# Two-layer streaming-encoder trunk on one core: the second layer's values projected token-major for four heads at a time

## The chip, the core and the metric

The kernel runs on one core of a Trainium2 chip. The metric is the device time of one execution in microseconds (us). The engines work side by side and wait for one another on semaphores: PE (TensorE) multiplies matrices, DVE (VectorE) and ACT (ScalarE) work element by element, POOL (GpSimd) clears buffers and issues some DMAs, SP (SyncE) issues the others. A matmul of PE takes a stationary operand of 128 x 128, which a separate load puts in place (PEld in the profile), and a moving operand of up to 512 columns, which streams past it; the product is summed in PSUM, which has eight banks of 128 x 512 float32.

## The reference, cut to what matters

The model has two layers over 512 tokens of width 1024. The change lies at the border between them: after the first layer the keys and values that the second layer reads are projected from the normalised stream, and each of 12 heads of width 64 attends over all earlier chunks.

```
ks_, vs_ = jnp.split(rmsnorm(x, kv_norm_g) @ w_kv, 2, axis=-1)      # (512, 1024) @ (1024, 1536)
...
s = jnp.einsum('bqhd,bkhd->bhqk', qc, kc).astype(jnp.float32) * scale + bias
s = jnp.where(valid, s, -jnp.inf)
p = jax.nn.softmax(s, axis=-1).astype(vc.dtype)
return jnp.einsum('bhqk,bkhd->bqhd', p, vc)
...
def rmsnorm(x, g):
    y = x32 * lax.rsqrt(jnp.mean(x32 * x32, axis=-1, keepdims=True) + EPS)
    return (y * g.astype(jnp.float32)).astype(x.dtype)
```

The factor of the norm is one number per token, so it can be applied to a projection's output in place of its input. The kernel does that: the input of the projection, `kvact`, holds x times the gain `kv_norm_g` only.

## The kernel before

**Numbers in two parts.** Every matmul operand is held as a high and a low part (`split`, L139: ACT casts the high part, L140; DVE subtracts it from the source, L141). A product is three matmuls, high by high, high by low, low by high (`mm3`, L192 to L196), summed in one PSUM bank.

**The stream is held feature-major.** `xT[j]`, j = 0 to 7, has 128 features on the partitions and the 512 tokens along the columns. A projection (`project`, L198) makes 128 output features by 512 tokens: it loads the weights' 128 columns for all eight feature blocks (512 KB, one DMA on SP's queue into a `wr` buffer), casts them into two weight tiles, and runs 8 steps of `mm3` with the weights stationary and the 512 tokens moving. One "step" below is one `yield` of this loop: three matmuls of 512 columns.

**Weight tiles** (`weight_tiles`, L160). There are three blocks, 0, 1 and 2, each a `wh` and a `wl` tile. Without an argument the blocks are taken in turn (`turn[0]`); with `block=` a given one is taken. Blocks 0 and 1 have 64 bytes (`HALF`, 16 floats) to spare, and which end is left free depends on the caller:

```
at = HALF if i < 2 and (block is None) == (tag == "wh") else 0
```

Counted in units of 64 bytes and in the order of the tags in `sizes` (L82 to L84), a tile of tag `u` begins at an even unit, `wh0` and `wh1` at an odd one, `wl0` and `wl1` at an even one. So weights that are taken in turn lie at even units, like `u`; weights with `block=` given lie at odd units, 64 bytes off `u`. The forms of the first layer's channel mixer use `block=0` and `block=1` (L903, L906) and multiply by activations in `u`, with the weights stationary.

**The border between the layers.** The last part of the first layer's down projection runs in a loop over j = 0 to 7 (L1283): weights of 128 x 768 from the rotating blocks, 18 matmuls of 512 columns, the sum added to `xT[j]`, its squares added to the norm's sum, and two scaled copies in two parts each, `kvact[j]` and `act[j]`, all in `u` tiles. `u` has 50 tiles, of which these 32 stay in use. Then `norm.finish` (L291) makes `norm.row`: 128 equal rows of 512, the norm's factor of each token; it is given projection steps to run beside it.

**The second layer's mixer.** A generator named `fill` runs six calls of `project_pair(j)` (two heads each), with the two memory-query projections before and after the sixth. In `project_pair` there are 24 steps: 8 for the values' projection `ov`, 8 for the keys', 8 for the queries'. The values come out feature-major, while the attention needs them with the tokens on the partitions. So DVE multiplies `ov` by `norm.row` (`times_row`, L1312) into a `t` tile, PE turns it by four transposes of 128 x 128 into a PSUM bank (L1323), and two `split`s write it into two tiles of 128 x 512 (L1328): for each head 64 columns of high part and 64 of low part. The tiles are one `fh` and one `fl` (four of each) for pairs 0 to 4, and two `u` for pair 5. Queries go through `queries` (L569) into four `u` tiles, keys through `head_keys` (L531) into two.

`band_attention(j)` (L1333) has 10 stages: scores and softmax for each of four groups of tokens, transposes of the probabilities, products with the values. `weave` (L225) lets a given number of `fill` steps run between its stages: 1.68, 1.826, 1.633 and 1.848 for pairs 0 to 3, 3.456 for pair 4; `until` runs `fill` until a pair is there. After pair 3 `load_memory_kv(1)` (L546) puts four more tiles into `u`, and `memory_attention` 0 waits for the memory queries (four `u`). Later the output projection's parts take the place of `fill`, beside memory attention 1 and pair 5.

PSUM's banks are tagged: three `mm` for projections, three `sc`, two `tr`.

**Order.** In the channel mixers and the first stage the order on PE, ACT and DVE is written by hand (`manual_schedule`). In the border and the second mixer it is not: a planner places each instruction by the program's order as its priority and by a model of when operands and free tiles will be there, and the order of each engine is then fixed. Instructions marked `pin` keep their order.

Of the kernel before, what the change touches and what calls it, by code (L numbers as in the profile page):

```python
# [10 lines left out]
F32R = mybir.dt.float32r  # L11
I32 = mybir.dt.int32
AF = mybir.ActivationFunctionType
ALU = mybir.AluOpType
AX = mybir.AxisListType

P = 128
D = 1024
S = 512
# [30 lines left out]
def f(ap):  # L50
    return ap.bitcast(F32)
# [3 lines left out]
def trunk(  # L55
# [34 lines left out]
    def sb(tag, shape, dtype=F32):  # L90
        count[0] += 1
        return pool.tile(shape, dtype, tag=tag, name=f"{tag}{count[0]}", bufs=bufs[tag])

    def ps(tag):
        count[0] += 1
        return psum.tile([P, S], F32, tag=tag, name=f"p{tag}{count[0]}", bufs=pbufs[tag])
# [42 lines left out]
    def split(hi, lo, src, on_act=True, pinned=False):  # L139
        high = A.copy(hi, src) if on_act else V.tensor_copy(hi, src)  # L140
        low = V.tensor_tensor(out=lo, in0=src, in1=f(hi), op=ALU.subtract)  # L141
        if pinned:
            pin(high)
            pin(low)

    def load(src, a, b, extra=None):
        n = b + (extra.shape[-1] if extra is not None else 0)
        raw = sb("wr", [P, D])[:, : a * n].rearrange("p (a b) -> p a b", a=a)
        if isinstance(src, list):
            for i, one in enumerate(src):  # L150
                nc.sync.dma_start(raw[:, i, :], one)
        else:
            nc.sync.dma_start(raw[:, :, :b], src)
        if extra is not None:
            nc.sync.dma_start(raw[:, :, b:], extra)
        return raw
# [17 lines left out]
    def parts(raw, pinned=False, block=None):  # L174
        _, a, b = raw.shape
        hi, lo = weight_tiles(a, b, block)
        split(hi, lo, raw, pinned=pinned)
        return hi, lo
# [6 lines left out]
    def weights(*args):  # L185
        return parts(load(*args))

    def rows(w, c0, n, k0=0, k1=None):
        k1 = k1 if k1 is not None else w.shape[0] // P
        return w[k0 * P : k1 * P, c0 : c0 + n].rearrange("(k p) c -> p k c", p=P)  # L190

    def mm3(o, lh, ll, rh, rl, first, last, more=False):  # L192

        nc.tensor.matmul(o, lh, rh, start=first, stop=False, skip_group_check=more)  # L194
        nc.tensor.matmul(o, lh, rl, start=False, stop=False, skip_group_check=more)  # L195
        nc.tensor.matmul(o, ll, rh, start=False, stop=last, skip_group_check=more)  # L196

    def project(w, c0, act, tag="mm"):  # L198


        n = len(act)
        wh, wl = weights(rows(w, c0, P), n, P)
        o = ps(tag)
        for k in range(n):
            mm3(o, wh[:, k, :], wl[:, k, :], act[k][0], act[k][1], k == 0, k == n - 1)
            yield
        return o
# [323 lines left out]
    def head_keys(t):  # L531
        ks = [sb("u", [P, S], F32R) for _ in range(2)]
        for h, r in enumerate(HEADS):
            A.copy(ks[h][r, :], t[r, :])
            V.tensor_tensor(out=ks[h][HEADS[1 - h], :], in0=t[r, :], in1=f(ks[h])[r, :], op=ALU.subtract)
        return ks
# [744 lines left out]
    logarithms()  # L1281
    norm2, kvact, act = Norm(), [], []
    for j in range(KT):  # L1283
        wh, wl = weights(rows(ffn_w_down[0], j * P, P, FT - LAST, FT), LAST, P)
        o = ps("mm")
        for k in range(LAST):
            mm3(o, wh[:, k, :], wl[:, k, :], *hid[k], k == 0, k == LAST - 1)
        V.tensor_add(xT[j], xT[j], o)
        norm2.add(xT[j])
        kvact.append(scaled(xT[j], col["gkv"][:, j : j + 1]))  # L1290
        act.append(scaled(xT[j], col["gmix"][:, 8 + j : 9 + j]))
        G.dma_start(xspill[j], xT[j])
# [12 lines left out]
    def blocks(pt, o, step, n):  # L1305
        a = pt[:, o : o + P]
        return bass.AP(tensor=a.tensor, offset=a.offset, ap=[list(a.ap[0]), [step, n], [1, P]])

    def project_pair(j):
        def times_row(o):  # L1310
            t = sb("t", [P, S])
            V.tensor_tensor(out=t, in0=o, in1=norm.row, op=ALU.mult)  # L1312
            return t

        ov = yield from project(w_kv, AW + j * P, kvact)
        t = times_row(ov) if norm.row is not None else None
        o = yield from project(w_kv, j * P, kvact)
        if t is None:
            t = times_row(ov)
        k = head_keys(times_row(o))  # L1320
        tp = ps("mm")
        for T in range(TT):
            nc.tensor.transpose(tp[:, T * P : (T + 1) * P], t[:, T * P : (T + 1) * P], ident)  # L1323
        v = []
        for i in range(2):

            w = sb("u" if j == 5 else ("fh", "fl")[i], [P, S], F32R).rearrange("p (h c) -> p h c", h=4)
            split(w[:, :, :HD], w[:, :, HD:], tp[:, i * MEM : (i + 1) * MEM].rearrange("p (h c) -> p h c", h=4))  # L1328
            v += [w[:, :2, :], w[:, 2:, :]]
        q = queries((yield from project(b_w_in, j * P, act)), norm.row)  # L1330
        qkv[j] = q, k, v

    def band_attention(j, q, k, v):  # L1333
        pts = [sb("pt", [P, 5 * S], F32R) for _ in range(2)]
# [203 lines left out]
```

## Time and profile before

| | |
|---|---|
| median of three runs | 1180.86 us (1180.71 to 1181.27) |
| the profiled execution | 1181.04 us, with a span of 1179.3 us from first to last instruction |
| last products of the first channel mixer end | about 581.5 us |
| down-projection loop, j = 0 to 7 | about 577.5 to 613.4 us |
| first and last of the values' transposes (L1323) | 625.1 and 749.5 us |
| first scores of the second mixer's band attention | about 634 us |
| last products with the values | 803.7 us |

The page of the profile gives, for each engine, the time in which it was busy and its share of the span. Matmuls are pipelined: one of 512 columns is listed with about 390 ns, and the next begins about 227 ns after it, so the price of a matmul is read from the distance between starts, not from its own duration. Idle time is listed with what ended it; idle time of an engine that is not the bottleneck costs nothing.

### The profile page before, as it was taken

To read this page: it belongs to the slowest core of one execution; us is meant where nothing else is said; L and a number is where in the kernel's file an instruction comes from. 1 tells how busy PE (TensorE), PEld (TensorE's weight loads), DVE (VectorE), ACT (ScalarE), POOL (GpSimd) and SP (SyncE) were. 2 spreads that over 40 slices of the span, in tenths; PEclk is the share of its full clock that TensorE was granted. 3 is DMA by queue.
4 is the path that set the end of the run, shared out by engine and by line. 5 is a ranking of instruction groups with operands and counts; after the bars stand their busy time and mean duration, and the time that the engine had idled before them with its cause. 6 is when DMAs were issued, how large, how long until landed. Compare 5 with 4: busy or idle time off the path is not lost.

```text
span 1179.3 us, 18676 instructions
## 1 busy us (share of the span) xinstructions
PE 1169.1 (99%) x7007; PEld 1034.2 (88%) x7007; DVE 935.7 (79%) x1688; ACT 725.8 (62%) x1294; POOL 129.9 (11%) x222
## 2 busy tenths in 40 slices
PE   9999999999999999999999999999999999999997
PEld 9988888888889999999888888888889999999986
DVE  6877788887978877777698888897897877777755
ACT  6548677654655655555666667776565655555545
POOL 1111101000021111111020000101001011111100
PEclk9999999999999999999999999999999999999999
DMA  8645325244266677765564312335426466666551
GB/s 299 208 109 134 94 55 152 76 139 121 90 166 163 164 164 162 164 148 129 150 200 125 90 54 85 106 102 177 139 90 153 108 143 144 143 143 141 123 158 72
DMA packets 200156, 158.64 MB, mean 135 GB/s; under 512 B 8344, under 2 KB 179838, under 8 KB 200066
## 3 DMA queue, kind: packets, MB, share of 16 engines
q1 hardware_dynamic: 183906, 119.74, 34.6%
q0 software_dynamic: 15584, 36.67, 16.4%
q8 instruction: 55, 0.90, 0.3%
q10 hardware_dynamic: 576, 1.05, 0.2%
q14 instruction: 35, 0.29, 0.1%
HBM read 128.89 MB, written 32.46 MB: 137 GB/s over the span
## 4 chain that ended last, share of the span: by engine, by line
PE 94%; DVE 3%; ACT 1%; issue 0%; DMA 0%; SPq 0%; POOL 0%; ACTq 0%; POOLq 0%; DVEq 0%
PE pmm L194 18%; PE pmm L195 18%; PE pmm L196 18%; PE ptr L195 6%; PE ptr L194 6%; PE ptr L196 6%; PE psc L195 5%; PE psc L196 5%; PE psc L194 5%; PE psc L544 2%; PE ptr L1365 1%; PE ptr L1386 1%; PE ptr L1387 1%; PE ptr L627 1%; PE ptr L613 0%; DVE pt L141 0%
## 5 line engine op out<-in xcount | busy, mean ns | idle before, releaser
L194 PE MATMUL pmm<-u,wh 128*128 128x512 f32 (+1 forms) x968 | 333.2, 345 | 0.4 <-ACT u L140 0.2
L196 PE MATMUL pmm<-u,wl 128*128 128x512 f32 (+1 forms) x968 | 330.8, 342 | 0.0
L195 PE MATMUL pmm<-u,wh 128*128 128x512 f32 (+1 forms) x968 | 330.5, 342 | 0.0
L141 DVE TENSOR_TENSOR wl<-wr,wh 128x1024 fp32r<-128x1024 f32 (+3 forms) x172 | 199.6, 1162 | 101.8 <-ACT wh L140 101.4
L140 ACT CAST wh<-wr 128x1024 fp32r<-128x1024 f32 (+3 forms) x172 | 172.0, 1002 | 92.7 <-PE pmm L195 39.0
L196 PEld LDWEIGHTS pmm<-u,wl 128*128 128x128 f32 x968 | 181.9, 188 | 20.6
L194 PEld LDWEIGHTS pmm<-u,wh 128*128 128x128 f32 x968 | 181.8, 188 | 19.3 <-ACT u L140 1.1
L195 PEld LDWEIGHTS pmm<-u,wh 128*128 128x128 f32 x968 | 182.0, 188 | 18.5 <-DVE u L141 0.5
L194 PE MATMUL ptr<-u,wh 128*128 128x512 f32 x272 | 106.7, 392 | 0.0
L195 PE MATMUL ptr<-u,wh 128*128 128x512 f32 x272 | 106.5, 392 | 0.0
L196 PE MATMUL ptr<-u,wl 128*128 128x512 f32 x272 | 105.8, 389 | 0.0
L778 POOL DMA_DIRECT2D xspill<-t x64 | 55.6, 869 | 447.3 <-ACT t L777 437.5
L141 DVE TENSOR_TENSOR fl<-pt,fh 128x512 fp32r<-128x512 f32 x102 | 70.3, 689 | 11.2 <-ACT fh L140 8.5
L194 PE MATMUL pmm<-u,fh 128*128 128x256 f32 x272 | 75.4, 277 | 0.0
L195 PE MATMUL pmm<-u,fh 128*128 128x256 f32 x272 | 75.2, 276 | 0.0
L196 PE MATMUL pmm<-u,fl 128*128 128x256 f32 x272 | 75.2, 276 | 0.0
L195 PE MATMUL psc<-u,wh 128*128 128x256 f32 (+1 forms) x232 | 75.1, 324 | 0.0
L196 PE MATMUL psc<-u,wl 128*128 128x256 f32 (+1 forms) x232 | 75.1, 324 | 0.0
L194 PE MATMUL psc<-u,wh 128*128 128x256 f32 (+1 forms) x232 | 75.0, 324 | 0.0
L140 ACT CAST fh<-pt 128x512 fp32r<-128x512 f32 x102 | 62.7, 615 | 13.5 <-DVE pt L888 13.3
L950 ACT ACTIVATE t<-t 128x512 f32<-128x512 f32 x34 | 21.5, 632 | 79.2 <-DVE t L685 79.2
L777 ACT COPY t<-ptr 128x512 f32<-128x512 f32 x64 | 37.6, 587 | 51.6 <-PE ptr L196 51.6
(335 smaller groups left out, 2540.3 us busy)
## 6 DMA issues: line engine op xcount, KB each, us to landing
wr<-in_ffn_w_up_dram SPq DMA_DIRECT2D x54, 512.0 KB, 5.0
wr<-in_ffn_w_down_dram SPq DMA_DIRECT2D x38, 512.0 KB, 4.1
pt<-in_ffn_w_up_dram SPq DMA_DIRECT2D x34, 512.0 KB, 6.9
xspill<-t POOLq DMA_DIRECT2D x64, 256.0 KB, 4.7
wr<-in_a_w_in_dram SPq DMA_DIRECT2D x20, 512.0 KB, 3.8
wr<-in_w_kv_dram SPq DMA_DIRECT2D x12, 512.0 KB, 4.0
xspill<-fh POOLq DMA_DIRECT2D x16, 256.0 KB, 2.6
xspill<-fl POOLq DMA_DIRECT2D x16, 256.0 KB, 3.0
```

The source lines that it names most:

```text
L140: high = A.copy(hi, src) if on_act else V.tensor_copy(hi, src)
L141: low = V.tensor_tensor(out=lo, in0=src, in1=f(hi), op=ALU.subtract)
L194: nc.tensor.matmul(o, lh, rh, start=first, stop=False, skip_group_check=more)
L195: nc.tensor.matmul(o, lh, rl, start=False, stop=False, skip_group_check=more)
L196: nc.tensor.matmul(o, ll, rh, start=False, stop=last, skip_group_check=more)
L544: nc.tensor.matmul(o, a, b, start=first and i == 0, stop=i == 1)
L627: nc.tensor.matmul(o2, vs[a][:, 2 * hp + h, :], p[h][:, a, :], start=i == 0, stop=i == 3)
L777: A.copy(t, o)
L778: G.dma_start(xspill[j], t, accum_op=ALU.add)
L950: A.activation(self.acc, self.acc, AF.Silu)
L1365: nc.tensor.transpose(tp[:, b * P : (b + 1) * P], es[T, h][:, b * P : (b + 1) * P], ident)
L1386: nc.tensor.matmul(o2[:, s * P :], w, hi_at(pts[h], s, s, TT - s), start=s == 0, stop=False)
```

## The change

In place of one feature-major projection of the values for each pair of heads there is `token_values(g)`, called for pairs 0, 2 and 4, which projects the values of four heads (256 columns of `w_kv`) at once with the tokens on PSUM's partitions. The activations `kvact` are the stationary operand, 128 tokens at a time, and the weights move past in 256 columns. Two `mm` banks hold the four groups of tokens, two in each. The weights are two loads of 128 x 1024, given to blocks 0 and 1 by name, and stay there for both halves of the 16 steps; a step is now two `mm3` of 256 columns. The tokens now lie on the partitions, so the norm's factor is needed as a column: once, four `tensor_tensor_reduce` multiply `norm.row`'s blocks of 128 x 128 by the identity and sum each row, into `acol`, a tile of the first layer. ACT then writes the high part scaled by that column, and DVE the low part, straight from PSUM into four tiles: `fh` for the first call, `fl` for the second, `u` for the third. The transposes, the multiplication by the row and the bank for them are gone. In the down-projection loop the turn of the blocks is moved on by one at j = 1 and j = 3.

```diff
     for j in range(KT):
+        turn[0] += j in (1, 3)
         wh, wl = weights(rows(ffn_w_down[0], j * P, P, FT - LAST, FT), LAST, P)
...
+    vcol, vals = [], []
+
+    def token_values(g):
+
+        banks = [ps("mm").rearrange("p (i c) -> p i c", i=2) for _ in range(2)]
+        ws = []
+        for i in range(2):
+            for k in range(KT):
+                if i == 0 and k % 4 == 0:
+                    ws.append(parts(load(rows(w_kv, AW + g * MEM, MEM, k, k + 4), 4, MEM), block=k // 4))
+                wh, wl = ws[k // 4]
+                for b, o in enumerate(banks):
+                    T = 2 * i + b
+                    lh, ll = (t[:, T * P : (T + 1) * P] for t in kvact[k])
+                    mm3(o[:, i, :], lh, ll, wh[:, k % 4, :], wl[:, k % 4, :], k == 0, k == KT - 1)
+                yield
+        if not vcol:
+            vcol.append(acol[:, 0, :])
+            for T in range(TT):
+                V.tensor_tensor_reduce(
+                    out=sb("t", [P, S])[:, :P], in0=norm.row[:, T * P : (T + 1) * P], in1=ident, scale=1.0, scalar=0.0,
+                    op0=ALU.mult, op1=ALU.add, accum_out=vcol[0][:, T : T + 1],
+                )
+        vals.append([])
+        for T in range(TT):
+            w = sb(("fh", "fl", "u")[g], [P, S], F32R).rearrange("p (h c) -> p h c", h=4)
+            c, o = vcol[0][:, T : T + 1], banks[T % 2][:, T // 2, :].rearrange("p (h c) -> p h c", h=4)
+            A.activation(w[:, :, :HD], o, AF.Copy, scale=c)
+            V.scalar_tensor_tensor(w[:, :, HD:], o, c, f(w[:, :, :HD]), op0=ALU.mult, op1=ALU.subtract)
+            vals[g].append(w)
+
     def project_pair(j):
-        def times_row(o):
-            t = sb("t", [P, S])
-            V.tensor_tensor(out=t, in0=o, in1=norm.row, op=ALU.mult)
-            return t
-
-        ov = yield from project(w_kv, AW + j * P, kvact)
-        t = times_row(ov) if norm.row is not None else None
+        if j % 2 == 0:
+            yield from token_values(j // 2)
         o = yield from project(w_kv, j * P, kvact)
-        if t is None:
-            t = times_row(ov)
-        k = head_keys(times_row(o))
-        tp = ps("mm")
-        for T in range(TT):
-            nc.tensor.transpose(tp[:, T * P : (T + 1) * P], t[:, T * P : (T + 1) * P], ident)
-        v = []
-        for i in range(2):
-
-            w = sb("u" if j == 5 else ("fh", "fl")[i], [P, S], F32R).rearrange("p (h c) -> p h c", h=4)
-            split(w[:, :, :HD], w[:, :, HD:], tp[:, i * MEM : (i + 1) * MEM].rearrange("p (h c) -> p h c", h=4))
-            v += [w[:, :2, :], w[:, 2:, :]]
+        t = sb("t", [P, S])
+        V.tensor_tensor(out=t, in0=o, in1=norm.row, op=ALU.mult)
+        k = head_keys(t)
         q = queries((yield from project(b_w_in, j * P, act)), norm.row)
-        qkv[j] = q, k, v
+        qkv[j] = q, k, [w[:, j % 2 * 2 : j % 2 * 2 + 2, :] for w in vals[j // 2]]
```

## The prediction, made before the changed kernel was seen

> **What bounds the kernel now.** I read the page first, then the busy time by stage, the starts of single matmuls, the groups by line and shape, and the waits of PE's weight loads.
>
> ```profile
> span 1179.3 us, 18676 instructions
> ...
> PE 1169.1 (99%) x7007; PEld 1034.2 (88%) x7007; DVE 935.7 (79%) x1688; ACT 725.8 (62%) x1294; POOL 129.9 (11%) x222
> ...
> PE 94%; DVE 3%; ACT 1%; issue 0%; DMA 0%; SPq 0%; POOL 0%; ACTq 0%; POOLq 0%; DVEq 0%
> ```
>
> PE is busy 99% of the span and 94% of the chain that ended last. The busy time by stage (columns: window, its length, busy us of PE, weight loads, DVE, ACT, POOL; then clock and DMA) says the same of the stretches that the change touches: from the last down product to the first attention, the attentions of pairs 0 to 3, and the rest of the mixer.
>
> ```profile
> 613.00:641.00 28.00, 28.00 (x134) 23.33 (x133) 22.41 (x46) 15.85 (x31) 4.71 (x9) 1.00 0.46 141
> 641.00:742.00 101.00, 100.90 (x517) 84.44 (x516) 83.82 (x205) 68.10 (x148) 6.26 (x12) 1.00 0.30 89
> 742.00:806.00 64.00, 63.42 (x343) 51.80 (x342) 57.15 (x153) 48.23 (x123) 6.04 (x11) 1.00 0.33 100
> ```
>
> PE is full in all three; DVE follows with 80%, 83% and 89%. So a change here is worth what it takes from PE's stream, as long as DVE and the chains of the softmax keep up. How much PE waits there is in the waits of its weight loads from 614 to 812 us (waiting, on whom, us, times, longest):
>
> ```profile
> PEld ptr L613 <- issue: 1.0, 4, 0.4
> PEld ptr L1365 <- issue: 1.0, 4, 0.4
> PEld ptr L1365 <- DVE pt L141: 0.7, 2, 0.4
> PEld psc L544 <- ACT t L601: 0.6, 2, 0.5
> PEld ptr L1386 <- DVE pt L141: 0.6, 2, 0.3
> PEld ptr L627 <- DVE pt L141: 0.5, 1, 0.5
> ```
>
> The six longest sum to 4.4 us. There is little waiting for the change to remove, and covered waiting that it could uncover.
>
> **Removed from PE: the transposes.** Starts of PE's matmuls around the first group:
>
> ```profile
> 624.83 0.39 PE L196 MATMUL pmm<-u,wl 128*128 128x512 f32 x1
> 625.06 0.60 PE L1323 MATMUL pmm<-ident,t 128*128 128x128 f32 x4
> 625.42 0.47 PE L194 MATMUL pmm<-u,wh 128*128 128x512 f32 x1
> 625.73 0.39 PE L195 MATMUL pmm<-u,wh 128*128 128x512 f32 x1
> ...
> L1323 PE MATMUL pmm<-ident,t x24: 270/273/273, 625.1 to 749.5; 128*128 128x128 f32 x24
> ```
>
> From 624.83 to 625.73 lie two matmuls of 512 columns and four transposes; the first matmul after the transposes is late, as 0.31 us lie behind its start. Plain matmuls of 512 columns follow at
>
> ```profile
> 609.81 0.39 PE L195 MATMUL pmm<-u,wh 128*128 128x512 f32 x1
> ...
> 613.89 0.39 PE L195 MATMUL pmm<-u,wh 128*128 128x512 f32 x1
> ```
>
> 4.08 us for 18, 0.2267 us each. So a group costs 0.90 - 0.45 = 0.45 us, and six (24 transposes) 2.7 us. This is the gain that I am surest of.
>
> **Changed on PE: the products.** Six projections of 24 matmuls of 512 columns (144) become three calls of 96 of 256 (288): the same columns, twice the instructions and weight loads. No matmul of before has these operands at these places, so I bound the price from two sides (first and last of a run):
>
> ```profile
> 570.66 0.28 PE L194 MATMUL pmm<-u,wh 128*128 128x256 f32 x1
> ...
> 577.47 0.40 PE L194 MATMUL pmm<-u,wh 128*128 128x512 f32 x1
> ...
> 1170.00 0.28 PE L194 MATMUL pmm<-wh,u 128*128 128x256 f32 x1
> ...
> 1172.04 0.28 PE L196 MATMUL pmm<-wh,u 128*128 128x256 f32 x1
> ```
>
> In the channel mixer's step, weights stationary and 64 bytes off the moving `u`, 60 matmuls take 6.81 us: 113.5 ns, half of 227. In the last stage the activations are stationary and the weights move, as in the change, but both lie at even units: 17 take 2.04 us, 120 ns. The change has the roles of the second and the offset of the first. I take 113.5 ns: what differs between the rows besides the roles is the offset, and it should not matter which of two operands is the odd one. Then 288 x 113.5 ns = 32.7 us against 144 x 226.7 ns = 32.6 us: nothing. At 120 ns it is 34.6 us, 1.9 us more; that end stays for the range. The Trainium skill, "TensorE: Matmul & The Clock Gate", section "Back-to-back issue gap", gives N / 2.4 + 2.5 ns between matmuls of N columns, a fixed part that speaks against halving them; my estimate by it is 144 x 2.5 ns = 0.4 us more. The rows show no such part: 113.5 is half of 227.
>
> **DVE, ACT, SP.**
>
> ```profile
> L1312 DVE TENSOR_TENSOR t<-pmm,rb 128x512 f32<-128x512 f32 x12 | 8.2, 681 | 1.2 <-PE pmm L196 1.1
> L1350 DVE CUSTOM_DVE_ANT_0 t<-psc,bias 128x128 f32<-128x128 f32 x12 | 3.4, 286 | 0.7 <-PE psc L544 0.6
> L1350 DVE DVE_READ_ACCUMULATOR2_ANT s<- 128x1 f32 x48 | 3.9, 82 | 0.0
> L141 DVE TENSOR_TENSOR fh<-pmm,fh 128x256 fp32r<-128x256 f32 x5 | 2.1, 420 | 0.1
> L140 ACT CAST fh<-pmm 128x256 fp32r<-128x256 f32 x5 | 1.9, 374 | 0.1
> ...
> wr<-in_w_kv_dram SPq DMA_DIRECT2D x12, 512.0 KB, 4.0
> ```
>
> Six of the twelve multiplications by the row go: 4.1 us of DVE. Four reductions come, by the attention's own of that shape 4 x (286 + 82) ns = 1.5 us, once. The evictions stay twelve of 128 x 256 on each engine, now with a scale: 374 and 420 ns, with no row for a dearer form; twice that would be 9.5 us over both engines, spread over three calls. Weight loads and casts stay six of 512 KB on SP, two in a bunch where one came per pair. All this lies beside PE. Without that cover the four reductions and four evictions, about 1.5 + 4 x 0.42 = 3.2 us, would hold the queries' projection of pair 0, which needs one of the two `mm` banks: three banks, two held by the call, the third by the keys. The keys' 8 steps last 8 x 3 x 0.227 = 5.4 us, so it is covered. The reductions wait for `norm.row`, which comes when the eleventh of the sixteen steps is through, as `norm.finish` yields 7.4 and 4; behind them on DVE stand these evictions and the next weight subtraction, which has 5.4 us. The keys of pair 0 come after the row.
>
> **The turn of the blocks.** Products 2, 3 and 4 of the down loop now reuse the block of the product but one before, so their cast cannot run two ahead. It does not now:
>
> ```profile
> 586.85 0.83 ACT L140 CAST wh<-wr 128x768 fp32r<-128x768 f32 x1
> 587.08 0.69 DVE L1288 TENSOR_TENSOR fh<-fh,pmm 128x512 f32<-128x512 f32 x1 [0.81 <-DMA fl<-xspill]
> ...
> 589.57 0.82 ACT L140 CAST wh<-wr 128x768 fp32r<-128x768 f32 x1
> 589.75 0.68 DVE L1288 TENSOR_TENSOR fh<-fh,pmm 128x512 f32<-128x512 f32 x1
> ```
>
> The third cast starts as the first product's sum is added, the fourth as the second's is. I take nothing; were each of the three late by its cast, 0.8 us, it would be up to 2.5 us. In the second channel mixer's first projections the turn moves likewise, with 5.4 us for each cast.
>
> **Steps moved.** The fill has 160 steps before and after, but pair 0 now needs 32 and not 24. So attention 0 starts 8 steps, 5.4 us, later, and these are missing as cover later. How many arrive there is a matter of `u` tiles. Before, at memory attention 0, 32 (`kvact`, `act`) + 8 (four outputs) + 6 (pair 4) + 4 (`load_memory_kv`) = 50 are in use, and its queries need 4 more, which come free when the keys of pair 5 have used `kvact` 0 and 1:
>
> ```profile
> 736.59 0.69 DVE L574 SCALAR_TENSOR_TENSOR t<-pmm,rb 128x512 f32<-128x512 f32 x1
> ...
> 741.12 0.52 POOL L524 MEMSET u<- 64x512 f32 x1 [22.14 <-PE pmm L195]
> 741.37 0.63 ACT L525 ACTIVATE u<-t 64x512 fp32r<-64x512 f32 x1
> ...
> 742.02 0.62 ACT L528 CAST u<-u 64x512 fp32r<-64x512 f32 x1
> ...
> 742.70 0.38 PE L544 MATMUL psc<-u,u 128*128 128x256 f32 x1
> ```
>
> The queries are out of PSUM at 736.6, the first clear waits until 741.1, the scores start at 742.7. After, the third call has put four more tiles into `u`, so pair 4's queries wait too, and ahead of the memory's: ACT has 2 x (two of 0.63 us and two copies like them) = 5 us to do where 2.5 sufficed. Memory attention 0 then starts with some 15 of the 160 steps left in place of about 20. Those 5 steps, 3.4 us, are PE work done earlier, not lost: the stretch from 742 runs beside less of the projections and more of the output projection's parts, which do not depend on them. DVE has 1.5 us less to do there (pair 5's row 0.68, two evictions 0.84). I put down 0.2 us of new waiting, with -1 and +5.4 us as ends.
>
> **Sum:** -2.7 + 0 + 0.2 = -2.5 us against 1181.04 us of the profiled execution (span 1179.3 and 1.7 around it) is 1178.5. That execution lies 0.2 above the median of 1180.86, so I predict **1178.4 us**, with 1177.4 to 1179.4 for this case alone. What a measurement of this kernel can tell from no change is about 0.2%, 2.4 us: the forecast lies on that line.
>
> **Rivals.**
> 1. *The offset does nothing with the roles exchanged.* The row at 1170 us speaks for it: these are its roles, at 120 ns. Against: there the units agree. +1.9: 1180.3 us, the same within what can be told.
> 2. *DVE's relief shows.* 2.6 us less DVE where it is busy 83 to 89%, and half of the 4.4 us of PE's waits go as well: 1176.2 us. Against: most of these waits are on the attention's own steps.
> 3. *The cover is missing at the end: slower.* Place: memory attention 0 to the attention of pair 5. If pair 4's queries hold the queue of ACT and the softmax chains then run at their own pace, the 8 steps moved stand as idle PE time: 5.4 us, 1178.4 + 5.2 = 1183.6 us. It decides from 2.7 us of new waiting on. For it: DVE at 89% there, and `u` full. Against: the parts of the output projection can be pulled forward.
> 4. *The load of the stationary operand sets the spacing.* It takes 188 ns in the row below; were it not hidden, 288 x (188 - 113.5) ns = 21.5 us come on top: 1199.9 us. Against: the 60 matmuls at 113.5 ns have loads of the same length.
>
> ```profile
> L195 PEld LDWEIGHTS pmm<-u,fh 128*128 128x128 f32 x272 | 51.1, 188 | 1.2
> ```
>
> The same section of the Trainium skill says that loads and matmuls together set the spacing, 81 ns at 128 columns and 131 at 512; my estimate between them, 98 ns at 256, would make the change 9 us slower. The trace does not agree: 227 ns at 512, 113.5 at 256.
>
> **How the numbers follow.** Forecast 0.42, split by the line into 0.26 faster and 0.16 the same; rival 1 0.10, the same; rival 2 0.19, faster; rival 3 0.26, of which 0.02 the same and 0.24 slower; rival 4 0.03, slower. Faster 0.45, the same 0.28, slower 0.27. The range goes from 1175.2, 1 us beyond rival 2, to 1184.8, 1.2 us beyond rival 3; rival 4 and a longer loss stay outside.
>
> **What would show it.** Right: no rows of L1323; the 288 matmuls 113 to 114 ns apart; PE as busy as now from the first step to 806 us; all later stages 2 to 3 us earlier. Wrong: 120 ns between them (rival 1); PE idle before products with the values or transposes after memory attention 0, waiting for DVE or ACT (rival 3); a gap at the third to fifth down product (the turn); the queries of pair 0 waiting for a bank.

## The result, and the profile after

The changed kernel takes 1182.91 us (median of 22 runs, 1181.87 to 1183.74), the kernel before 1181.00 us in the same runs (1180.37 to 1183.07). The ratio is 1.0015, with a 95% interval of 1.0008 to 1.0022: 1.9 us slower, where 2.5 us faster was forecast. The time lies inside the predicted range and on the other side of no change. The profiled execution took 1182.67 us, with a span of 1181.0 us.

From the page of the kernel after, its span, the busy times and the chain that ended last:

```profile
span 1181.0 us, 18909 instructions
...
PE 1168.3 (99%) x7127; PEld 1038.9 (88%) x7127; DVE 933.9 (79%) x1690; ACT 725.9 (61%) x1294; POOL 129.2 (11%) x222
...
PE 92%; ACT 3%; DVE 3%; issue 1%; DMA 0%; SPq 0%; POOL 0%; DVEq 0%; ACTq 0%; POOLq 0%
```

PE has 0.8 us less to do than before (1169.1), and yet the span is 1.7 us longer: work went, and more waiting came. Where it came stands in the busy time by stage, in the three stretches of the prediction:

```profile
613.00:641.00 28.00, 28.00 (x173) 25.19 (x172) 19.73 (x36) 14.82 (x23) 4.71 (x9) 1.00 0.47 147
641.00:742.00 101.00, 100.92 (x610) 88.86 (x609) 85.60 (x219) 68.83 (x156) 6.06 (x12) 1.00 0.33 101
742.00:806.00 64.00, 61.32 (x328) 49.48 (x327) 56.00 (x150) 47.70 (x122) 5.77 (x11) 1.00 0.24 71
```

Up to 742 us PE is as full as it was. From 742 to 806 us it is busy for 61.32 us in place of 63.42: 2.1 us of new idle time. The waits of the weight loads from 614 to 812 us, the seven longest:

```profile
PEld psc L544 <- ACT u L528: 1.1, 1, 1.1
PEld ptr L613 <- issue: 1.0, 2, 0.8
PEld ptr L1383 <- issue: 1.0, 4, 0.5
PEld psc L544 <- DVE s L1368: 0.9, 1, 0.9
PEld psc L544 <- ACT pt L140: 0.9, 1, 0.9
PEld ptr L1404 <- DVE pt L141: 0.8, 4, 0.3
PEld ptr L613 <- PE pmm L196: 0.7, 1, 0.7
```

(L1383 is the line of L1365 before, L1404 that of L1386, L1368 that of L1350.) Before, no single wait was longer than 0.5 us; now five are of 0.7 us or more, and they stand at the scores of the attentions (L544) and at the memory attentions' transposes (L613).

For the experiments I measure one stage between two instructions that all kernels have: from the last sum of the first down projection to the first sum of the second output projection (L658). It begins at times up to 2.8 us apart in executions of the same lines (613.47 to 616.28 us), so the stage says more than the position. The starts in the kernel before:

```profile
613.87 0.69 DVE L1288 TENSOR_TENSOR fl<-fl,pmm 128x512 f32<-128x512 f32 x1
...
810.68 0.69 DVE L658 TENSOR_TENSOR fh<-fh,pmm 128x512 f32<-128x512 f32 x1 [1.61 <-PE pmm L196]
```

and in the kernel after:

```profile
614.19 0.69 DVE L1289 TENSOR_TENSOR fl<-fl,pmm 128x512 f32<-128x512 f32 x1
...
811.91 0.69 DVE L658 TENSOR_TENSOR fh<-fh,pmm 128x512 f32<-128x512 f32 x1 [1.93 <-PE pmm L196]
```

That is 196.81 us before and 197.72 us after. The sums of the windows cut at these instructions give PE's busy time in the stage, before:

```profile
sum 196.81, PE 196.13 PEld 162.72 DVE 164.17 ACT 134.41 POOL 17.02; mean PE 98.07 PEld 81.36 DVE 82.09 ACT 67.21 POOL 8.51
```

and after:

```profile
sum 197.72, PE 194.96 PEld 167.43 DVE 162.66 ACT 134.87 POOL 16.54; mean PE 97.48 PEld 83.71 DVE 81.33 ACT 67.43 POOL 8.27
```

PE works 1.17 us less and idles 2.76 us in place of 0.68, 2.08 us more: together 0.91 us longer. Of the span's other 0.8 us, 0.3 us are there ahead of the stage and 0.5 us come behind it, in code that is the same but for the turn of the blocks; both are less than what lies ahead of the stage varies by.

### The profile page after: what moved, and what is told of

The parts are those of the page before. It is cut to its first block, busy times and chain, and to the rows that moved or that the text cites. A ratio compares the mean times of both kernels' runs of the same rounds, so it can differ in the third digit from the quotient of the medians.

```text
span 1181.0 us, 18909 instructions
## 1 busy us (share of the span) xinstructions
PE 1168.3 (99%) x7127; PEld 1038.9 (88%) x7127; DVE 933.9 (79%) x1690; ACT 725.9 (61%) x1294; POOL 129.2 (11%) x222
## 3 DMA queue, kind: packets, MB, share of 16 engines
q10 hardware_dynamic: 576, 1.05, 0.2%
## 4 chain that ended last, share of the span: by engine, by line
PE 92%; ACT 3%; DVE 3%; issue 1%; DMA 0%; SPq 0%; POOL 0%; DVEq 0%; ACTq 0%; POOLq 0%
PE pmm L194 18%; PE pmm L195 18%; PE pmm L196 17%; PE ptr L195 6%; PE ptr L194 6%; PE ptr L196 6%; PE psc L195 5%; PE psc L196 5%; PE psc L194 5%; PE psc L544 2%; PE ptr L1383 1%; PE ptr L1404 1%; PE ptr L1405 1%; ACT u L525 0%; PE ptr L613 0%
## 5 line engine op out<-in xcount | busy, mean ns | idle before, releaser
L194 PE MATMUL pmm<-u,wh 128*128 128x512 f32 (+1 forms) x920 | 314.0, 342 | 0.3 <-ACT u L140 0.2
L195 PE MATMUL pmm<-u,wh 128*128 128x512 f32 (+1 forms) x920 | 311.6, 339 | 0.2 <-DVE u L141 0.2
L196 PE MATMUL pmm<-u,wl 128*128 128x512 f32 (+1 forms) x920 | 311.1, 338 | 0.0
L141 DVE TENSOR_TENSOR wl<-wr,wh 128x1024 fp32r<-128x1024 f32 (+3 forms) x172 | 199.5, 1162 | 94.8 <-ACT wh L140 94.3
L196 PEld LDWEIGHTS pmm<-u,wl 128*128 128x128 f32 x920 | 172.8, 188 | 19.5 <-DVE wl L141 0.3
L194 PEld LDWEIGHTS pmm<-u,wh 128*128 128x128 f32 x920 | 172.7, 188 | 17.9 <-ACT u L140 1.1
L195 PEld LDWEIGHTS pmm<-u,wh 128*128 128x128 f32 x920 | 173.0, 188 | 17.4 <-DVE u L141 1.1
L195 PE MATMUL ptr<-u,wh 128*128 128x512 f32 x272 | 106.5, 392 | 0.0
L141 DVE TENSOR_TENSOR fl<-pt,fh 128x512 fp32r<-128x512 f32 x102 | 70.3, 689 | 11.1 <-ACT fh L140 8.5
L195 PE MATMUL pmm<-u,fh 128*128 128x256 f32 x272 | 75.2, 276 | 0.0
L195 PE MATMUL psc<-u,wh 128*128 128x256 f32 (+1 forms) x232 | 75.2, 324 | 0.0
```

## The experiments

All results in one table; "stage" is the stretch just defined in the one profiled execution, and "before" the kernel before on the same chip. A stage length is one sample each; I read none finer than about 1 us. The intervals of two runs that overlap do not tell them apart.

| run | what it is | us | before | ratio, 95% interval | stage, us |
|---|---|---|---|---|---|
| after | the change | 1182.91 | 1181.00 | 1.0015, 1.0008 to 1.0022 | 197.7 |
| e_order | before, steps in the order of after | 1185.29 | 1180.88 | 1.0036, 1.0023 to 1.0049 | 201.0 |
| e_pool | before, pair 4's values in `u` | 1185.90 | 1181.21 | 1.0041, 1.0028 to 1.0053 | 201.0 |
| e_order_fh | e_order, third group in `fh` | 1187.04 | 1181.21 | 1.0050, 1.0037 to 1.0062 | 202.5 |
| e_fh | after, third call in `fh` | 1183.90 | 1180.88 | 1.0029, 1.0018 to 1.0041 | 198.8 |
| e_kq | after, keys and queries ahead of the values | 1186.37 | 1180.88 | 1.0045, 1.0031 to 1.0059 | 202.1 |
| e_noturn | after, without the turn | 1184.23 | 1181.21 | 1.0029, 1.0018 to 1.0039 | 198.9 |
| e_even | after, weights at even units | 1182.82 | 1181.01 | 1.0016, 1.0007 to 1.0025 | 198.1 |
| v_m0 | after, memory queries earlier | 1181.96 | 1180.90 | 1.0008, 1.0000 to 1.0017 | 197.3 |
| v_m0_fh | v_m0 and e_fh | 1182.06 | 1180.90 | 1.0009, 1.0000 to 1.0018 | 197.3 |
| b_m0 | before, memory queries earlier | 1182.34 | 1180.90 | 1.0012, 1.0003 to 1.0021 | 198.2 |
| w_m0_r2 | v_m0, lower rate | 1182.34 | 1181.01 | 1.0005, 0.9996 to 1.0014 | 197.6 |
| w_m0_fh_r2 | v_m0_fh, lower rate | 1181.42 | 1181.01 | 1.0005, 0.9996 to 1.0013 | 196.9 |
| w_m0_r2_l3 | w_m0_r2, more cover at the end | 1182.92 | 1181.01 | 1.0011, 1.0002 to 1.0020 | 198.7 |
| x_turn | w_m0_fh_r2, weight blocks turned | 1180.44 | 1180.75 | 0.9999, 0.9990 to 1.0007 | 195.9 |
| x_turn_m1 | x_turn, other rates | 1181.22 | 1180.75 | 1.0004, 0.9995 to 1.0013 | 196.8 |

### Order or form

The change does two things at once: it gives the products another form, and it moves steps, two pairs' values ahead of the first pair's keys. e_order does the second without the first. It is the kernel before, transposes and all, with the projections of two pairs' values back to back; the value tiles are laid as in after, so pair 4's lie in `u` too:

```diff
-        ov = yield from project(w_kv, AW + j * P, kvact)
...
+        if j % 2 == 0:
+            ovs = []
+            for jj in (j, j + 1):
+                ovs.append((yield from project(w_kv, AW + jj * P, kvact)))
+            for jj, ov in zip((j, j + 1), ovs):
+                t = times_row(ov)
...
+                    w = sb(("fh", "fl", "u")[j // 2], [P, S], F32R).rearrange("p (h c) -> p h c", h=4)
```

> The kernel before, with the order of the steps alone changed: for pairs 0, 2 and 4 the values of two pairs are projected back to back (16 steps), feature-major with transposes as before, third group in u. PE's work is that of before. If the steps moved and the full u pool are what cost (theory 1): PE waits about 3 us more than before, +2 to +4 us, 1183 to 1185. If the cost of the change lies in the new products alone (theory 2): within 0.7 us of before.

It took 1185.29 us, 4.4 more than before. Its stage:

```profile
613.96:742.09 128.13, 127.07 (x641) 105.36 (x640) 103.63 (x247) 79.93 (x174) 9.18 (x17) 1.00 0.36 109
742.09:814.98 72.89, 70.26 (x367) 56.83 (x366) 60.69 (x157) 54.05 (x129) 7.35 (x14) 1.00 0.30 86
sum 201.02, PE 197.33 PEld 162.19 DVE 164.32 ACT 133.98 POOL 16.52; mean PE 98.67 PEld 81.09 DVE 82.16 ACT 66.99 POOL 8.26
```

The instructions of PE are those of before (641 + 367 matmuls, as 645 + 363 there), and PE idles 3.7 us in place of 0.7; another 1.2 us are busy time, since short waits between matmuls count as busy while a matmul is listed longer than the distance to the next. So the order, with the tiles that go with it, costs 4.2 us of the stage, and the form, which is what after has beyond it, gives 3.3 back (201.0 to 197.7; 2.5 by the two ratios). Most of its waits are those of after, with the same lengths at the same places (of the weight loads, from 614 to 816 us; L1355 is the softmax's line, L1368 in after):

```profile
PEld psc L544 <- DVE s L1355: 2.0, 3, 0.9
...
PEld psc L544 <- ACT u L528: 1.1, 1, 1.1
...
PEld psc L544 <- ACT pt L140: 0.9, 1, 0.9
PEld ptr L613 <- PE pmm L196: 0.7, 1, 0.7
PEld pmm L195 <- DVE u L141: 0.6, 1, 0.6
```

Behind 742 us PE idles six times for more than 0.15 us in both kernels, 0.63, 0.38, 0.48, 0.27, 0.59 and 0.19 us in after, and 0.64, 0.36, 0.48, 0.27, 0.58 and 0.19 us in e_order, each some 3 us later. The first of them in e_order (after's is shown further down), then the fifth, in after and in e_order:

```profile
747.90 0.50 PE L544 MATMUL psc<-u,u 128*128 128x256 f32 x2 [0.64 <-ACT u L528]
...
792.42 0.62 PE L544 MATMUL psc<-u,u 128*128 128x384 f32 x2 [0.59 <-DVE s L1368]
...
795.45 0.61 PE L544 MATMUL psc<-u,u 128*128 128x384 f32 x2 [0.58 <-DVE s L1355]
```

This is the run that settles the sign: the waits behind 742 us come with the order, whatever the form of the products, and the new form by itself gains. What e_order has beyond them lies ahead of 742 us, where after has no such wait: 0.35 us at its transposes and 0.33 us each at two scores.

e_kq puts the moved steps elsewhere: `token_values` behind the keys and queries of the even pair, whose attention waits for the values only at its products. The first scores then start at 629.1 us; before it was 634.4, in after 640.1.

```diff
     def project_pair(j):
...
+        qkv[j] = q, k
         if j % 2 == 0:
             yield from token_values(j // 2)
-        o = yield from project(w_kv, j * P, kvact)
...
+        until(lambda: len(vals) > j // 2, fill)
```

> The changed kernel with keys and queries of an even pair projected ahead of its 16 value steps, which then run beside that pair's own attention; it starts 16 steps earlier and the steps serve as cover later. Theory 1 with the moved steps as its main part: waits fall by 2 to 4 us, to 1179 to 1181. If the pool decides: no change from 1182.9 within 1 us, as the same tiles are full at memory attention 0.

1186.37 us, worse by 3.5 us than after; neither expectation was met. Starting the attentions earlier does not help in this order; 1.3 us of its waits are for the cast of a weight block (PE idles 0.88 us for it at 741.9 us), of which after has none.

### The tiles in `u`

The wait of 1.1 us at the first scores of memory attention 0 is the one that the prediction described. The timeline of after from 738.5 to 746 us shows it, first POOL (start, length, engine, line; in brackets the idle time before it):

```profile
739.94 0.52 POOL L524 MEMSET u<- 64x512 f32 x1 [65.33 <-PE pmm L195]
...
741.98 0.52 POOL L524 MEMSET u<- 64x512 f32 x1 [0.16 <-PE pmm L195]
743.34 0.52 POOL L524 MEMSET u<- 64x512 f32 x1 [0.84 <-PE pmm L195]
744.02 0.52 POOL L524 MEMSET u<- 64x512 f32 x1 [0.16 <-PE pmm L195]
```

Then the last of ACT's instructions there:

```profile
743.49 0.63 ACT L525 ACTIVATE u<-t 64x512 fp32r<-64x512 f32 x1
744.15 1.26 ACT L528 CAST u<-u 64x512 fp32r<-64x512 f32 x2
```

And PE:

```profile
743.79 0.39 PE L196 MATMUL pmm<-u,wl 128*128 128x512 f32 x1
744.82 1.38 PE L544 MATMUL psc<-u,u 128*128 128x256 f32 x8 [0.63 <-ACT u L528]
```

Six clears from 739.94 on, for pair 4's queries and the memory's, each as soon as the keys of pair 5 (`pmm`, L195) have let go of `kvact`; the first of ACT's last two copies is through by 744.8, and PE, whose last product began at 743.79, waits for it. The wait of the weight load is 1.05 us, of which PE is idle for 0.63. The question is whether this wait is the loss. e_fh puts the third call into `fh`, which makes it go. `reload_x` writes `fh` too and has to come later for it; what that costs by itself no run shows.

```diff
-            w = sb(("fh", "fl", "u")[g], [P, S], F32R).rearrange("p (h c) -> p h c", h=4)
+            w = sb(("fh", "fl", "fh")[g], [P, S], F32R).rearrange("p (h c) -> p h c", h=4)
...
     run(fill)
-    reload_x()
...
+    reload_x()
     run(chain(fill, outp.part(0, 5), outp.part(1, 5)))
```

> The changed kernel with the third call's values in the four fh tiles, free by then, in place of u, and the reload of x moved behind the attention of pair 5. The u pool then holds 54 and not 58 tiles at memory attention 0, as before. Theory 1 with the u pool as its main part: the wait of 1.0 us ahead of the first scores of memory attention 0 goes, and the time falls by 1 to 2 us, to 1181 to 1182. If the missing steps cost and not the pool: the time stays at 1182.9 within 0.7 us.

The wait went, and the kernel took 1183.90 us, 1.0 us over after; neither expectation was met. The waits of e_fh:

```profile
PEld psc L544 <- DVE s L1368: 2.6, 3, 2.2
...
PEld pmm L195 <- DVE u L141: 1.4, 1, 1.4
```

A wait of 2.2 us stands at the second group of pair 5's scores and one of 1.4 us at the output projection. e_order_fh does the same to e_order:

> e_order with the third group's values in fh and not u, and the reload of x behind the attention of pair 5: the order of the steps alone, without the fuller pool. If the order costs: +3 to +5 us over before, as e_order's +4.4. If the pool costs: +0 to +1.5 us.

1187.04 us, again not faster. e_pool is the reverse: the kernel before, in its own order, with pair 4's two value tiles in `u` too:

```diff
-            w = sb("u" if j == 5 else ("fh", "fl")[i], [P, S], F32R).rearrange("p (h c) -> p h c", h=4)
+            w = sb("u" if j >= 4 else ("fh", "fl")[i], [P, S], F32R).rearrange("p (h c) -> p h c", h=4)
```

> The kernel before with one change: pair 4's values in two u tiles, as pair 5's, in place of fh and fl, so that two more u tiles are held at memory attention 0 with the steps in their old order. If the full u pool costs by itself: +0.5 to +2 us over before. If the order of the steps is what costs: within 0.5 us of before.

1185.90 us, 4.7 more than before, from where two tiles lie, about as much as the steps moved cost in e_order, and more than either expectation had. PE around its longest wait:

```profile
791.67 1.09 PE L627 MATMUL ptr<-pt,u 128*128 128x512 f32 x4
794.58 0.50 PE L544 MATMUL psc<-u,u 128*128 128x256 f32 x2 [1.82 <-DVE s L1350]
```

The wait is some 50 us behind the memory's queries, where the tiles are short, at pair 5's scores, on a softmax of DVE. The same one stands in e_fh and e_order_fh, where `u` has to hold four tiles less than in after: PE idles 1.81, 1.83 and here 1.82 us. In all three DVE's order has the subtraction of a weight block of 128x768 (L141, 0.96 us) and two instructions of L564 (1.39 us together) ahead of the first step of pair 5's softmax; in after that subtraction stands behind it. So an edit at one place changes what the planner puts first at another, and removing the first visible wait moves the loss and does not remove it.

### The spacing of the products

The 288 matmuls of 256 columns in after, first and last of the stretch behind the norm's two matmuls in the first call, 53 spacings:

```profile
619.41 0.28 PE L194 MATMUL pmm<-wh,u 128*128 128x256 f32 x1
...
625.65 0.28 PE L196 MATMUL pmm<-wh,u 128*128 128x256 f32 x1
```

6.24 us / 53 = 117.7 ns: neither the 113.5 that I took nor the 120 of the other end. Three runs measure it by itself: they compute nothing of the reference, only rows of 96 matmuls with the operands at chosen places (0 bytes means that they begin a multiple of 512 bytes apart). The first has both roles and several offsets (16 to 128 bytes), the second the sign of the offset, the third the place itself and the same case twice.

> Leaves out the whole computation: only matmuls in runs of 96, with activations or weights stationary and the weights at 0, 16, 32, 48, 64, 96 or 128 bytes off the activations. Theory A (the offset rule holds for both roles, and the changed kernel's 117.8 ns come from what runs beside it): weights stationary 120 ns at 0 and 113.5 at 64 bytes; activations stationary the same, 120 and 113.5. Theory B (the roles differ): activations stationary 120 at 0 and about 118 at 64 bytes, while weights stationary gives 113.5 at 64. 512 columns: 227 ns at either offset.

> Leaves out the whole computation: runs of 96 matmuls as in m_spacing, now with the high and the low part of the weights on different sides of the activations' place (counted modulo 512 bytes, where the channel mixer's step has high -64, low +64, and so has the changed kernel). Theory C: what counts is the place of the stationary operand being loaded against the moving one streaming at that time. In the mixer's step that runs -64, +64, -64; with the roles exchanged the same places give +64, -64, +64. Then weights stationary at (-64, +64) gives 113.5 ns, activations stationary at (+64, -64) gives 113.5 and at (-64, +64) 117.8. Theory D: the roles decide: activations stationary gives 117 to 118 at all of these, weights stationary at (-64, +64) 113.5. 512 columns at (-64, +64): 227 to 235.

> Leaves out the whole computation: eighteen runs of 96 matmuls of 256 columns, some twice, at places of the weights that m_spacing and m_spacing2 had. m_spacing gave 117.8 ns for weights stationary with both parts at +64 bytes, m_spacing2 113.3 for all three offsets 512 bytes further on, and 113.5 for activations stationary with the parts at -64 and +192. Theory E (the places decide, over more than 512 bytes): repeated places repeat their spacing within 0.3 ns wherever they stand in the run, weights stationary at 64/64 is 117.8 and at 576/576 113.3, activations stationary at 448/704 is 113.5 again. Theory F (something drifts with time or the instruction stream): the repeats differ.

| 96 matmuls, mean of 95 spacings in ns | 0 bytes | high part 64 bytes off |
|---|---|---|
| activations stationary, 256 columns | 120.0 | 117.7 to 117.8 in most, 113.5 in two, 117.0 and 118.9 in one each |
| weights stationary, 256 columns | 119.9 to 120.0 | 117.7 to 117.8 in three, 113.3 to 113.4 in five |
| weights stationary, 512 columns | 226.8 | 233.3 to 233.4 |

The first run's other offsets gave 116.7 to 119.9 ns at 256 columns. Exchanging the roles leaves the values as they are: at 0 bytes both take 120.0 ns, and 64 bytes off both occur at 117.8 and at 113.4. What the prediction did not allow for is that one place has two spacings. In the third run the case with the high part at 448 and the low part at 704 bytes stands twice (L179 to L181, L332 to L334), first and last matmul of each:

```profile
79.62 0.28 PE L179 MATMUL pb<-w,u 128*128 128x256 f32 x1
...
90.81 0.28 PE L181 MATMUL pb<-w,u 128*128 128x256 f32 x1
...
203.51 0.29 PE L332 MATMUL pb<-w,u 128*128 128x256 f32 x1
...
214.29 0.28 PE L334 MATMUL pb<-w,u 128*128 128x256 f32 x1
```

11.19 us / 95 = 117.8 ns and 10.78 / 95 = 113.5 ns, with the same operands. The row of the channel mixer from which I took the price runs in the second way, the three calls in the first, in every variant here but e_even. What selects between them is open.

e_even asks what the offset is worth in the kernel: it puts the weights of the values at even units, where the activations lie.

```diff
-                    ws.append(parts(load(rows(w_kv, AW + g * MEM, MEM, k, k + 4), 4, MEM), block=k // 4))
+                    ws.append(parts(load(rows(w_kv, AW + g * MEM, MEM, k, k + 4), 4, MEM), block=k // 4, even=True))
```

> The changed kernel with the values' weights at the same units as the activations (both even) and not 64 bytes off; nothing else moves. The micro runs say 120.0 ns and not 117.8, 288 x 2.2 ns = 0.6 us: 1183.5 us, 0.6 over the changed kernel, with 120 ns between the matmuls of the three calls. If the full kernel's 117.8 ns had nothing to do with the offset: 117.8 ns and 1182.9.

The spacing went to about 119.5 ns, the three calls became 0.4 us longer together (11.84 + 17.34 + 16.78 against 11.65 + 17.24 + 16.64 us), and the time, 1182.82 us, cannot be told from after. So 64 bytes are worth about 0.5 us by the spacing, not 1.9.

### The turn of the blocks

e_noturn leaves out `turn[0] += j in (1, 3)`.

> The changed kernel without the line that moves the turn of the blocks at j = 1 and 3. The values' first block is then that of the fifth product and its second that of the last, which is used until the values' first step. If the turn is free, as predicted, and was needed: 0 to +1.5 us over the changed kernel, with a gap some four steps into the values. If the turn itself costs (later casts in the loop, and the second mixer's first projections): 0.3 to 1 us faster than the changed kernel's 1182.9.

1184.23 us, 1.3 more than after, though the intervals touch. PE of e_noturn at the start of the values:

```profile
616.10 0.39 PE L196 MATMUL pmm<-u,wl 128*128 128x512 f32 x1
617.44 0.50 PE L194 MATMUL pmm<-wh,u 128*128 128x256 f32 x2 [0.95 <-ACT wh L140]
```

Without the turn the first block of the values is the last one of the down projection, not that of its fifth product as I had expected, and its cast holds PE for 1.1 us (617.44 - 616.10, less one spacing of 0.23). That is about what the stage is longer by, 198.9 for 197.7. The turn costs nothing that shows in the down loop: from the loop's first sum (L1288, L1289 in after) to its last it takes 28.29 us before, 28.26 in after and 28.27 in e_noturn.

### Can the order be mended?

If the loss is order, another order should bring it back. v_m0 runs the first memory queries ahead of pair 4, where `u` is not full; v_m0_fh adds e_fh's edit; b_m0 does the same to the kernel before.

```diff
-    fill = chain(*(project_pair(j) for j in range(5)), b_memory_queries(0), project_pair(5), b_memory_queries(1))
+    fill = chain(*(project_pair(j) for j in range(4)), b_memory_queries(0), project_pair(4), project_pair(5), b_memory_queries(1))
```

> The changed kernel with the first memory queries projected ahead of pair 4, the third call's values still in u. If cover decides: 1 to 3 us faster than the changed kernel's 1182.9. If the u pool decides: no faster, as 52 tiles are wanted when memory attention 0's values are loaded.

> e_fh with the first memory queries projected ahead of pair 4, so that memory attention 0 can follow the attention of pair 3 and the steps of pairs 4 and 5 stand beside it and the two attentions after it. In the changed kernel PE has only projections from 730 to 744.8 us and DVE is at 70% there. Theory 1 (the end of the mixer lacks cover): waits behind 742 us fall by 2 to 4 us, 1179.5 to 1182. If the planner's order makes new waits whatever is moved: 1183 to 1187, as the four rearranged kernels so far.

> The kernel before with the first memory queries projected ahead of pair 4 and nothing else changed. If the kernel before has cover to spare and its order is merely one that fits: +2 to +5 us, as other rearrangements of it. If more cover at the end helps any kernel: 0 to -2 us.

1181.96 and 1182.06 us, about 1 us under after by the medians, with intervals that overlap its own; b_m0 is 1.4 us over before, and its interval leaves 1 out. An order that is no worse for the one form, and by the medians better, is a worse one for the other.

The next three lower the rate at which `fill` is used up beside pair 4, from 3.456 to 2.0 steps, so that cover is left for the last attentions; the third also moves the cover within the last pair (`weave(islice(job, 8), fill, 2.0, 3)`).

> v_m0 (first memory queries ahead of pair 4) with the rate of fill steps beside pair 4's attention lowered from 3.456 to 2.0, so that its 20 or so remaining steps last to its end. If the cover's place decides the waits of the end: waits there fall by 1 to 2 us, 1180 to 1181, at or under the kernel before. If the planner redistributes the work anyway: within 0.7 us of v_m0's 1182.0.

> v_m0_fh (values of the third call in fh, reload of x later) with the same lower rate of 2.0. Cover's place: 1180 to 1181. Otherwise within 0.7 us of v_m0_fh's 1182.1.

> w_m0_r2 with three output-projection steps ahead of pair 5's first scores and a rate of 2.0 in place of 2.372 behind them, so that the change from memory attention 1 to pair 5 is covered. Cover's place: 1179.5 to 1181. Otherwise within 0.7 us of w_m0_r2.

1182.34, 1181.42 and 1182.92 us: the intervals of the first two hold 1, the third gained a new wait at the output projection (PE idles 1.15 us there). In w_m0_fh_r2 the largest wait of PE ahead of 742 us was for the cast of a weight block that the memory queries had just used:

```profile
709.01 0.73 PE L544 MATMUL psc<-u,u 128*128 128x128 f32 x5
710.09 0.51 PE L194 MATMUL pmm<-wh,u 128*128 128x256 f32 x2 [0.35 <-ACT wh L140]
```

x_turn takes the other block there; x_turn_m1 changes two rates besides.

```diff
+        turn[0] += j == 3
         q = queries((yield from project(b_w_in, j * P, act)), norm.row)
...
     def b_memory_queries(hp):
+        turn[0] += hp == 0
```

> The kernel of w_m0_fh_r2 with the turn of the two weight blocks shifted once more before the queries projection of the fourth pair and once before the first memory queries. If the waits that remain at the end of the mixer are each a price of their own, the wait of 0.57 us for the recast of weight block 0 near 709 us goes and nothing comes for it: 1180.9, level with before (ratio 1.000, interval across 1). If waits only move, 1181.2 to 1181.9, as w_m0_fh_r2 was.

> x_turn with the planner rate beside the first memory attention 1.0 in place of 0.8 and beside the fifth pair 1.7 in place of 2.0, so that the cover is laid more evenly over the last two pairs. If the remaining waits come from cover that is spent too early, 1180.2 to 1180.9; if from the order of the vector work itself, 1181 to 1183.

In x_turn the wait is gone, and its stage is the shortest of all:

```profile
616.27:744.40 128.13, 127.44 (x781) 113.04 (x780) 106.66 (x260) 86.66 (x191) 11.82 (x22) 1.00 0.31 94
744.40:812.13 67.73, 67.25 (x348) 54.95 (x347) 55.49 (x146) 48.13 (x113) 4.82 (x10) 1.00 0.33 102
sum 195.86, PE 194.69 PEld 167.99 DVE 162.15 ACT 134.79 POOL 16.64; mean PE 97.35 PEld 83.99 DVE 81.07 ACT 67.39 POOL 8.32
```

PE idles 1.2 us, where after had 2.8 and before 0.7, with the busy time of after. 1180.44 us is 0.9999 of before (0.9990 to 1.0007): the loss is recovered, and no version here is shown to beat the kernel before. Its interval lies just under that of after (from 1.0008); of the steps on the way (queries earlier, values in `fh`, lower rate, other blocks) none is told from the one ahead of it. x_turn_m1, 1181.22 us, cannot be told from it.

## Why the prediction was wrong

**The bound.** Right: PE's stream set the time, and a change was worth what it took from it plus the idle time that it made.

**The transposes, -2.7 us.** Right as a mechanism: no such row is left, and e_order against after, the same order with and without them, differs by 2.5 us (by the ratios) to 3.3 us (by the stage) in spite of the dearer products. The 2.7 us by themselves no run measures.

**The products, 0.** Mis-sized: 117.7 ns in place of 113.5 are 288 x 4.2 ns = 1.2 us, within the bounds that I gave (0 to 1.9). The reason I gave for the lower end, that it does not matter which operand is the odd one, held; that a place has one spacing did not. So rival 1, with 1.9 us, was nearer in size than my nothing, and its reason, the roles, was wrong. Rival 4 is ruled out by the same rows: loads of 188 ns do not set the spacing. The Trainium skill, "TensorE: Matmul & The Clock Gate", section "Step-by-step: what each phase is for", says that the weights are read through a port of their own, so that loading them takes no read bandwidth from the running matmul; by that the place of the operands should not show. The runs here differ: 120.0 ns at 0 bytes, 113.4 or 117.8 at 64, though they do not show where in the path the difference arises.

**DVE, ACT, SP: hidden.** Right: PE is full from 613 to 641 us, and no wait stands at the queries of pair 0. DVE's total fell by 1.8 us, less than the 2.6 us worked out, since the scaled evictions are dearer than the rows I had: DVE 476 ns for 420, ACT about 480 for 374.

**The turn: nothing.** Right for the down loop (28.29 us before, 28.26 in after). Without it the values would wait 1.1 us for their first block, which the prediction did not say.

**Steps moved, 0.2 us: this step failed.** I took the steps moved for PE work done earlier, not lost. e_order prices the step in the old form, with the tiles laid as in after: 4.4 us. In after 2.1 us of new idle time stand from 742 to 806 us where I had put 0.2, at the place that rival 3 named, and the wait for pair 4's and the memory's queries in `u` came as described, at 1.05 us. But it is only the first of several, and e_fh shows that the rest does not hang on it. Rival 3, with a chance of 0.26, was right in its place and in the first wait. Its price was not met in after, where the new idle time is under the 2.7 us from which it was to decide; that its 1183.6 us lies 0.7 from the measured time is in part luck, since it is added to a forecast without the dearer products. What I weighed too lightly, though I had named it, is that PE was at 99.1% there and DVE at 89%. A lack of slack is not the whole of it: x_turn has the form and the busy time of after and idles 1.2 us, so these steps can be taken in by an order made for them. I took "can be pulled forward" for "will be in time", and the planner's order, fixed before the kernel runs, did not bring it.

**The sum.** In the stage: -2.7 (transposes) + 1.2 (products) + 2.1 (idle) = +0.6, measured +0.9; the 0.3 us between them are busy time, which fell by 1.2 us and not by 1.5. The remaining 0.8 us of the spans lie outside the stage; whether the change has a part in them is open. Open too is how the loss divides between the steps moved and the tiles in `u`, since e_pool's two tiles cost as much as e_order's steps, and why the planner's order makes these waits rather than others; that the order, with these tiles, makes them was shown.

## What to carry to other kernels

Split a change of form from the change of order that comes with it, and price the order by itself, in the old form: here it cost 4.4 us, and the form gained 2.5 to 3.3. Where PE is at 99% and its partner near 90%, moved steps are not free even if no instruction is added, and here a wait taken away at one place came back at another until cover was laid anew for the new form (rates, block turns, order of the queries). A spacing is best taken from a row with the same operands at the same places, and then still with both observed values as bounds.

## What the runs showed of the hardware

In the three runs, at a granted clock of 1.00, matmuls of 128 x 256 with a load each ran at 120.0 ns with the operands a multiple of 512 bytes apart, and with 64 bytes beside that mostly at 113.4 or 117.8 ns, with either role; the last two values occur with identical operands. At 512 columns it was the other way round: 226.8 ns at 0 bytes and 233.4 ns at 64. In the first of the three runs, 512 columns without and with the offset, first and last:

```profile
181.90 0.40 PE L302 MATMUL pb<-u,w 128*128 128x512 f32 x1
...
203.44 0.39 PE L304 MATMUL pb<-u,w 128*128 128x512 f32 x1
203.67 0.40 PE L314 MATMUL pb<-u,w 128*128 128x512 f32 x1
...
225.84 0.39 PE L316 MATMUL pb<-u,w 128*128 128x512 f32 x1
```

21.54 and 22.17 us for 95 spacings. The offset that helped one width harmed the other.
